# Pooling edges from gathered rows, and the mixer's instructions in another order

## The chip, the cores and the metric

One core of one Trainium2 chip runs the kernel. The core has engines that work side by side and each take their instructions strictly in the order of the program: TensorE (PE, matrix products into the eight PSUM banks), VectorE (DVE), ScalarE (ACT) and GpSimd (POOL). SyncE (SP) computes nothing here; its queue issues nearly all transfers between the device's memory (HBM) and the on-chip memory (SBUF). Engines wait for each other through semaphores. The metric is the device time of one execution in microseconds, lower is better. Times within the run are counted from the first instruction.

## The reference

A decoder trunk of two layers on 512 tokens with 1024 channels, all in float32. Layer 0 mixes tokens by pooling, layer 1 by sliding-window attention; a convolutional gated feed-forward network (FFN) follows each. The change lies in layer 0's mixer and in the start of its FFN:

```
def pool_mixer(h, w_pool, scale):      # h = rms_norm(x, mix_pre_g[0])
    # windows (2, 4, 8, 16), one for each group of 256 channels
    mean = (csum[:, 1:, sl] - csum[:, lo, sl]) / cnt      # causal trailing mean
    d = mean - hf[..., sl]
    y = einsum('bsgc,gcd->bsgd', d, w_pool)               # per group 256 x 256
    return y * scale

x = x + rms_norm(pool_mixer(h), mix_post_g[0])
f = conv_glu_ffn(rms_norm(x, ffn_pre_g[0]), ...)          # up-projection 1024 -> 2 * 2816 first
```

A token's trailing mean over up to 16 tokens reaches up to 15 tokens back, so the first tokens of a block of 128 need the last rows of the block before. These are the edges.

## The kernel before

The 512 tokens lie in four blocks (b = 0 to 3) of 128, the 1024 channels in eight chunks of 128; every chunk belongs to one of the four groups, two chunks to a group. The steps of the mixer are, for each block, with the names of the code and of the traces:

- **norm** (`mix_norm`): the mean square of x[b] in two halves (`ss_m`), three tiny steps on GpSimd that end in the reciprocal root (`rstd_end`, lines 285 and 286), and two VectorE products that write the normalised block `xm`.
- **pool** (`mix_pool`): for each chunk one float32 product of the block's rows with a banded 128 x 128 matrix (line 415), and for b > 0 one more product, 16 columns wide, of the *previous* block's whole 128 rows with the small edge matrix (line 416). Four chunks share a PSUM bank `pd`; ScalarE copies it to `d`. Block 0 has its own band and no edge (line 413).
- **map** (`mix_map`, line 426): eight products, 256 columns wide, with the pool weights `wp`, into two banks `my`. `wp` is the raw weight times the gain and the scale row (`mix_weights`, line 400); the scale row is spread over the partitions by two products with a matrix of ones (line 374).
- **post** (`mix_post`): the post norm and the sum into x[b], then **pre** (`mix_pre`): the norm for the FFN into `xn_f`, then **T** (`mix_T`, line 335): eight transposes, whose result is split into a high and a low part, `xTh` by ScalarE and `xTl` by VectorE.

The FFN's weights come in units of 1 MB (`load`, line 172, tile `raw`, two buffers). Each unit is split into a high part by ScalarE (`wh`) and a low part by VectorE (`wl`), for units 0 and 1 in quarters (`piece`, lines 214 and 220). The up-projection (`up`) makes every product three times (`mm3`, lines 342 to 344): high with high, high with low, low with high. In the mixer's stage it is made for two blocks at a time (256 columns), from the third unit on for all four (512 columns).

Before x arrives PE multiplies a matrix of ones with itself (`keep_busy`, line 369). SP loads, in this order: x[0] in two halves, the band for block 0, x[1], constants, the rest of the band, the pool weights in two halves, x[2], the post gain row (`mpost`), x[3], weight unit 0, the pre gain row (`fpre`, which takes the scale row's buffer), later constants, the convolution's constants, weight unit 1 (which takes the pool weights' buffer).

The order on PE, ScalarE, VectorE and GpSimd is that of the program text. SP alone is ordered by a planner from its own timing, among transfers whose buffers are free, the earlier in the text first. Buffers of one tag are handed out by the framework as they come free, which adds waits where a buffer is still in use.

Of the kernel before, what the change touches and what calls it, by code (L numbers as in the profile page):

```python
# [60 lines left out]
def _pieces(v, bits, n):  # L61
    out = []
    for _ in range(n - 1):
        q = 2.0 ** (math.floor(math.log2(v)) + 1 - bits)
        c = math.floor(v / q) * q
        out.append(c)
        v -= c
    out.append(float(np.float32(v)))
    return out


def build(nc, tc, ctx, a, out):
# [7 lines left out]
    def bank(name):  # L80
        return ps.tile([P, 512], F32, tag="ps", name=name)
# [20 lines left out]
    def gain_col(which, kc):  # L102
        o = C_GAIN + which * KC + kc
        return cst[:, o : o + 1]
# [58 lines left out]
    def load(i):  # L163
        if i in raws or i in ready or i >= N_UNITS:
            return
        r = pw.tile([P, 2048], F32, tag="raw", name=f"raw{i}", bufs=2)
        if U_K <= i < U_O:
            load_att(r, i, 0, 4)
            raws[i] = r
            return  # L170
        for o, src in source(i)[1]:
            nc.sync.dma_start(r[:, o : o + src.shape[1]], src)
        raws[i] = r
# [90 lines left out]
    def ahead(i, n=N_SLOTS):  # L264

        for k in range(i, i + n):
            split(k)
# [7 lines left out]
    def square(junk, src, ss, h, first):  # L275

        nc.scalar.activation(junk, src, AF.Square, scale=1.0 / math.sqrt(D), accum_out=ss[:, h : h + 1])  # L277
        if first:
            nc.gpsimd.tensor_scalar(ss[:, h : h + 1], ss[:, h : h + 1], EPS, None, ALU.add)  # L279

    def new_ss(name):
        return pc.tile([P, 4], F32, tag="ss", name=f"ss_{name}", bufs=6)

    def rstd_end(ss):
        nc.gpsimd.tensor_tensor(ss[:, 2:3], ss[:, 0:1], ss[:, 1:2], ALU.add)
        nc.gpsimd.tensor_tensor(ss[:, 3:4], ss[:, 2:3], mhalf, ALU.pow)
        return ss[:, 3:4]
# [8 lines left out]
    def halves(t):  # L296
        return [t[:, h * 512 : (h + 1) * 512] for h in range(2)]

    def post_norm(b, acc, grow, name, pool=None):
        if pool is None:  # L300
            ts_ = halves(pc.tile([P, D], F32, tag="t4", name=f"pt_{name}{b}", bufs=3))
        else:
            ts_ = [pool.tile([P, 512], F32, tag="qT", name=f"pt_{name}{b}_{h}", bufs=2) for h in range(2)]
        r = rstd_of(acc, ts_, f"p_{name}{b}")
        gs, xs = halves(grow), halves(x[b])
        for h in range(2):
            nc.vector.tensor_tensor(ts_[h], acc[h], gs[h], ALU.mult)
        for h in range(2):
            nc.vector.scalar_tensor_tensor(xs[h], ts_[h], r, xs[h], ALU.mult, ALU.add)
# [45 lines left out]
    nc.sync.dma_start(x[2], a["x"][2])  # L355
    post_row = bcast_row(a["mix_post_g"][0], "mpost0")
    nc.sync.dma_start(x[3], a["x"][3])
    load(U_IN[0])
    pre_row = bcast_row(a["ffn_pre_g"][0], "fpre0")
    load(U_IN[0] + 1)  # L360
    nc.sync.dma_start(cst[:, C_LATE:C_FREQ], a["cst"][:, C_LATE:C_FREQ])
    load_conv(0)
    scale_row = [bank(f"scale_row{h}") for h in range(2)]
    scratch = bank("scratch")

    def keep_busy(n):

        for _ in range(n):
            nc.tensor.matmul(scratch[:, :P], warm, warm, start=True, stop=True)

    keep_busy(13)

    for h in range(2):
        nc.tensor.matmul(scale_row[h], warm, row[:, h * 512 : (h + 1) * 512], start=True, stop=True)
    keep_busy(1)
    wp = pm.tile([P, 8, 256], F32, tag="wp", name="wp")
    xns, xnf = {}, {}

    def mix_norm(b):
        xm = pm.tile([P, D], F32, tag="xm", name=f"xm{b}", bufs=NB)  # L380
        ss = new_ss(f"m{b}")
        xs, junk = halves(x[b]), halves(xm)
        if b < 2:

            nc.scalar.activation(junk[0], xs[0], AF.Square, scale=1.0 / math.sqrt(D), accum_out=ss[:, 0:1])
            nc.vector.tensor_tensor_reduce(out=junk[1], in0=xs[1], in1=xs[1], scale=1.0 / D, scalar=EPS,
                                           op0=ALU.mult, op1=ALU.add, accum_out=ss[:, 1:2])
        else:
            for h in range(2):
                square(junk[h], xs[h], ss, h, h == 0)  # L390
        r = rstd_end(ss)
        for h in range(2):
            nc.vector.tensor_scalar(halves(xm)[h], halves(x[b])[h], r, None, ALU.mult)
        xns[b] = xm

    def mix_weights():
        pr = raws[U_POOL]
        for c in range(8):
            g = c // 2
            nc.vector.scalar_tensor_tensor(wp[:, c, :], pr[:, c * 256 : (c + 1) * 256], gain_col(0, c),  # L400
                                           scale_row[g // 2][:, (g % 2) * 256 : (g % 2 + 1) * 256], ALU.mult, ALU.mult)

    def mix_pool(b):
        d = pm.tile([P, D], F32, tag="d", name=f"d{b}", bufs=2)
        for h in range(2):
            pd = bank(f"pd{b}{h}")
            for k in range(4):
                c = h * 4 + k
                g = c // 2
                cs = slice(c * P, (c + 1) * P)  # L410
                o = pd[:, k * P : (k + 1) * P]
                if b == 0:
                    nc.tensor.matmul(o, xns[b][:, cs], band[:, g, P + EDGE :], start=True, stop=True)
                else:
                    nc.tensor.matmul(o, xns[b][:, cs], band[:, g, :P], start=True, stop=False)
                    nc.tensor.matmul(o[:, :EDGE], xns[b - 1][:, cs], band[:, g, P : P + EDGE], start=False, stop=True)
            nc.scalar.copy(d[:, h * 512 : (h + 1) * 512], pd)
        return d

    def mix_map(b, d):  # L420
        acc = [bank(f"my{b}{h}") for h in range(2)]
        for g in range(4):
            o = acc[g // 2][:, (g % 2) * 256 : (g % 2) * 256 + 256]
            for k in range(2):
                c = g * 2 + k
                nc.tensor.matmul(o, d[:, c * P : (c + 1) * P], wp[:, c, :], start=k == 0, stop=k == 1)  # L426
        return acc

    def mix_post(b, acc):
        post_norm(b, acc, post_row, "m0")  # L430

    def mix_pre(b):
        xnf[b] = pre_norm(b, pre_row, "f0")

    def mix_T(b):
        transpose_in(b, xnf[b], xT, "f0")

    u0, u1 = U_IN[0], U_IN[0] + 1
    mix_norm(0)
    mix_norm(1)  # L440
    d0 = mix_pool(0)
    mix_weights()
    mix_norm(2)
    d1 = mix_pool(1)
    acc0 = mix_map(0, d0)
    mix_post(0, acc0)
    mix_norm(3)
    acc1 = mix_map(1, d1)
    mix_pre(0)
    mix_post(1, acc1)  # L450
    d2 = mix_pool(2)
    piece(u0, 0)
    mix_T(0)
    mix_pre(1)
    piece(u0, 1)
    acc2 = mix_map(2, d2)
    piece(u0, 2)
    mix_post(2, acc2)
    d3 = mix_pool(3)
    mix_T(1)  # L460
    piece(u0, 3)
    mix_pre(2)
    acc3 = mix_map(3, d3)
    piece(u1, 0, defer=True)
    piece(u1, 1, defer=True)
    mix_post(3, acc3)
    while deferred:
        deferred.pop(0)()
    piece(u1, 2)
    piece(u1, 3)  # L470
    mix_pre(3)

    def start0():
        yield 0, (0, 2)
        mix_T(2)
        yield 1, (0, 2), (0,)
        mix_T(3)
        ctx_mix.close()
        yield 1, (0, 2), (1,)
        ahead(U_IN[0])  # L480
        rope_tables()
        yield 0, (2, 4)
        yield 1, (2, 4)


    sin_t = pc.tile([P, NB, 32], F32, tag="sin", name="sin_t")
# [29 lines left out]
        nc.scalar.activation(cos_t, ang, AF.Sin)  # L516


    def up(l, xT, j, accs, blks, sides=(0, 1)):
        hi, lo = slots[U_IN[l] + j]  # L520
        hi4 = hi.rearrange("p (k s c) -> p k s c", k=KC, s=2)
        lo4 = lo.rearrange("p (k s c) -> p k s c", k=KC, s=2)
        if j not in accs:
            accs[j] = [bank(f"u{l}_{j}_{s}") for s in range(2)]
        b0, b1 = blks
        for s in sides:
            o = accs[j][s][:, b0 * P : b1 * P].rearrange("p (b t) -> p b t", t=P)
            for k in range(KC):
# [694 lines left out]
```

## Time and profile before

| what | value |
|---|---|
| median of three runs | 910.92 us (910.71 to 912.18) |
| the profiled execution, its own time | 910.81 us |
| its span, first to last instruction | 909.0 us |
| PE busy | 900.4 us (99%) |
| DVE, ACT, POOL busy | 639.0, 457.9, 330.0 us |
| mean granted clock of PE | 0.999 |
| transfers over the span | 178.47 MB, mean 196 GB/s |

The page gives busy time by engine, the busy share of forty slices, the chain of work that ended last and the costliest groups. The end of a matmul in it is modelled, so a busy PE says less than its starts do: the distance from one start to the next is the time that a product takes. The views used below are the engines' rows in order of time (start, duration, engine, line, operation, tiles, count, and in brackets the idle time before with what ended it), the list of waits, the transfers from issue to landing, and busy time and granted clock in chosen stretches.

### The profile page before, as it was taken

What the parts mean: (1) busy time and instruction counts of PE and PEld (TensorE: products, weight loads), DVE (VectorE), ACT (ScalarE), POOL (GpSimd) and SP (SyncE); (2) the same over time, 40 slices, a digit from 0 to 9 for tenths busy, and PEclk for the clock granted to TensorE, in tenths of its full rate; (3) what the DMA queues carried; (4) which work ended last, traced back from release to release, by engine and by line L of the source; (5) the groups of instructions that cost most, each with busy time, mean ns of one, the idle gap of its engine ahead of it and who ended that gap; (6) DMA issues with size and microseconds to landing.
All of it is one profiled execution on the core that took longest, in us unless ns stands there. A gap on an engine that the chain in (4) does not pass through costs nothing.

```text
span 909.0 us, 12195 instructions
## 1 busy us (share of the span) xinstructions
PE 900.4 (99%) x4416; PEld 762.2 (84%) x4416; DVE 639.0 (70%) x949; ACT 457.9 (50%) x791; POOL 330.0 (36%) x360
## 2 busy tenths in 40 slices
PE   9999999999999999999999999999999999999996
PEld 8998888888888888888888889988888888888885
DVE  5987676676678679855988746655555555777897
ACT  5654444444444566545888635333333333455672
POOL 3418444444441003234655213544444444410031
PEclk9999999999999999999999999999999999999999
DMA  8257887888885666751211252555555555556562
GB/s 315 89 191 267 310 302 262 305 300 289 275 292 156 185 220 231 265 178 45 75 66 47 94 218 95 185 188 203 199 198 195 187 191 189 173 160 191 195 218 109
DMA packets 50207, 178.47 MB, mean 196 GB/s; under 512 B 5473, under 2 KB 13153, under 8 KB 42210
## 3 DMA queue, kind: packets, MB, share of 16 engines
q1 hardware_dynamic: 48272, 164.83, 52.3%
q10 hardware_dynamic: 1874, 12.85, 3.7%
q8 instruction: 35, 0.57, 0.3%
q14 instruction: 26, 0.21, 0.1%
HBM read 139.91 MB, written 37.75 MB: 195 GB/s over the span
## 4 chain that ended last, share of the span: by engine, by line
PE 96%; DVE 1%; DMA 1%; POOL 1%; ACT 0%; issue 0%; ACTq 0%; POOLq 0%; DVEq 0%
PE u L343 18%; PE u L342 18%; PE u L344 18%; PE dn L342 7%; PE dn L343 7%; PE dn L344 7%; PE op L342 2%; PE op L344 2%; PE op L343 2%; PE qp L343 2%; PE my L426 2%; PE qp L344 2%; PE qp L342 1%; PE pT L972 1%; DMA wl<-lo 1%; PE s L937 1%
## 5 line engine op out<-in xcount | busy, mean ns | idle before, releaser
L342 PE MATMUL u<-xTh_f,wh 128*128 128x512 f32 (+1 forms) x768 | 285.7, 372 | 0.0
L343 PE MATMUL u<-xTl_f,wh 128*128 128x512 f32 (+1 forms) x768 | 285.2, 371 | 0.0
L344 PE MATMUL u<-xTh_f,wl 128*128 128x512 f32 (+1 forms) x768 | 285.2, 371 | 0.0
L257 DVE TENSOR_TENSOR wl<-raw,wh 128x1024 fp32r<-128x1024 f32 (+1 forms) x158 | 206.6, 1338 | 33.0 <-ACT wh L256 32.6
L561 ACT ACTIVATE t<-u,conv 128x512 f32<-128x512 f32 x88 | 68.4, 780 | 250.3 <-PE u L344 219.4
L256 ACT CAST wh<-raw 128x1024 fp32r<-128x1024 f32 (+1 forms) x158 | 158.9, 1042 | 56.2 <-DMA raw<-t 41.4
L563 DVE SCALAR_TENSOR_TENSOR t<-u,conv,t 128x511 f32<-128x511 f32 x88 | 65.8, 747 | 147.7 <-ACT t L561 147.7
L342 PEld LDWEIGHTS u<-xTh_f,wh 128*128 128x128 f32 x768 | 144.6, 188 | 25.2
L344 PEld LDWEIGHTS u<-xTh_f,wl 128*128 128x128 f32 x768 | 144.6, 188 | 24.9
L343 PEld LDWEIGHTS u<-xTl_f,wh 128*128 128x128 f32 x768 | 144.6, 188 | 24.8
L582 POOL TENSOR_TENSOR G<-G,G 128x256 f32<-128x256 f32 x22 | 34.4, 1564 | 261.5 <-DVE G L577 261.5
L342 PE MATMUL dn<-wh,gh 128*128 128x512 f32 x276 | 107.6, 390 | 0.0
L344 PE MATMUL dn<-wh,gl 128*128 128x512 f32 x276 | 107.4, 389 | 0.0
L343 PE MATMUL dn<-wl,gh 128*128 128x512 f32 x276 | 107.4, 389 | 0.0
L279 POOL TENSOR_SCALAR ss_p_f<-ss_p_f 128x1 f32<-128x1 f32 x8 | 16.9, 2111 | 158.1 <-ACT dn L277 158.1
L564 DVE SCALAR_TENSOR_TENSOR t<-u,conv,t 128x510 f32<-128x510 f32 x88 | 65.9, 749 | 3.1
L344 PEld LDWEIGHTS dn<-wh,gl 128*128 128x128 f32 x276 | 51.8, 188 | 10.9
L342 PEld LDWEIGHTS dn<-wh,gh 128*128 128x128 f32 x276 | 51.8, 188 | 10.7
L343 PEld LDWEIGHTS dn<-wl,gh 128*128 128x128 f32 x276 | 51.8, 188 | 10.6
L948 ACT ACTIVATE P<-P,stat 128x256 f32<-128x256 f32 (+1 forms) x64 | 30.3, 476 | 11.4 <-DVE stat L945 11.3
L577 DVE TENSOR_TENSOR G<-t 128x512 f32<-128x512 f32 x44 | 32.3, 733 | 5.4 <-ACT t L571 1.0
L591 POOL TENSOR_TENSOR q<-q,q 128x512 f32<-128x512 f32 x22 | 33.0, 1502 | 4.3 <-PE tr_f L335 4.3
(193 smaller groups left out, 1380.6 us busy)
## 6 DMA issues: line engine op xcount, KB each, us to landing
raw<-in_ws_dram SPq DMA_DIRECT2D x46, 1024.0 KB, 5.0
q<-in_ws_dram SPq DMA_DIRECT2D x44, 512.0 KB, 6.1
raw<-t SPq DMA_DIRECT2D x24, 768.0 KB, 5.7
raw<-in_ws_dram SPq DMA_DIRECT2D x28, 512.0 KB, 4.8
t<-q SPq DMA_DIRECT2D x44, 256.0 KB, 2.8
t<-q SPq DMA_DIRECT2D x22, 512.0 KB, 2.8
hi<-h SPq DMA_DIRECT2D x12, 512.0 KB, 6.7
lo<-r SPq DMA_DIRECT2D x12, 512.0 KB, 5.9
```

Of the source, the lines that this page charges most:

```text
L256: nc.scalar.copy(hi[:, s], r[:, s])
L257: nc.vector.tensor_tensor(lo[:, s], r[:, s], hi[:, s].bitcast(F32), ALU.subtract)
L342: nc.tensor.matmul(acc, ah, bh, start=first, stop=False)
L343: nc.tensor.matmul(acc, ah, bl, start=False, stop=False)
L344: nc.tensor.matmul(acc, al, bh, start=False, stop=last)
L561: nc.scalar.activation(t, u, AF.Identity, bias=conv_col(l, ch, 3), scale=conv_col(l, ch, 2))
L563: nc.vector.scalar_tensor_tensor(t[:, 1:], u[:, : S - 1], conv_col(l, ch, 1), t[:, 1:], ALU.mult, ALU.add)
L564: nc.vector.scalar_tensor_tensor(t[:, 2:], u[:, : S - 2], conv_col(l, ch, 0), t[:, 2:], ALU.mult, ALU.add)
L577: nc.vector.tensor_tensor(g, tg, tv, ALU.mult)
L582: nc.gpsimd.tensor_tensor(s1, s1, G2[:, p, 2, :], ALU.add)
L591: nc.gpsimd.tensor_tensor(b22, b22, b12, ALU.subtract)
L948: nc.scalar.activation(Pt[:, h, 0:w], Pt[:, h, 0:w], AF.Exp, bias=nm[:, h : h + 1], scale=-1.0, accum_out=dn[:, h : h + 1])
```

## The change

**Edges.** The edge products of blocks 2 and 3 are replaced. A table `edge` of 128 x 8 x 16 is cleared on GpSimd and filled by eight small loads (16 rows of 16 numbers each), so that rows 16c to 16c+15 hold chunk c's edge matrix in chunk c's columns and zeros elsewhere. After block 1 is normalised, eight transfers within SBUF gather its last 16 rows, chunk c into rows 16c to 16c+15 of a tile `xe`; the same after block 2. One product of `xe` with four chunks' 64 columns of `edge` then adds the edges of four chunks to a bank at once. Block 1 keeps its eight narrow products. Only the first product into a bank of blocks 2 and 3 now starts it anew.

**Order.** The mixer's functions are taken apart into single steps, and a list of their names sets the order in which they are given out; as before, each engine takes its own in that order, and the transfers of `xe` go to SP. The first four up-projection parts (two units, two sides, two pairs of blocks, formerly 48 or 24 products at a time) are given out in quarters of six products. One filler product of PE behind the scale rows is gone; the scale rows are made one before and one behind the first half of pd0.

```diff
+MIXER = """
+    sqa0 sqa1 srow0 sqb0 rt0 xm00 xm01 sqb1 pd00 srow1 rt1 xm10 d00 xm11 pd01 wp3 d01 xe1 sqa2 wp2 pd10 wp5 sqb2
+    wp1 pd11 wp0 d10 wp7 wp4 sqa3 wp6 map00 eps2 psq00 rt2 xm20 xm21 eps3 peps0 ptt00 map01 xe2 psq01 map10 prt0
+    d11 wh00 ptt01 pd20 pst00 sqb3 map11 psq10 rt3 pst01 wl00 d20 nsq00 nsq01 psq11 pd21 wh10 xm31 xm30 wh01
+    map20 ptt10 d21 wh11 peps1 pd30 neps0 ptt11 nrt0 prt1 nst01 wh02 T01 psq20 nst00 pst10 T00 pd31 pst11 peps2
+    wl01 nsq10 neps1 wl10 map21 nsq11 d30 ptt20 th01 nrt1 tl01 map30 nst10 nst11 d31 T10 th00 wh12 psq21 T11
...
+    th30 th31 tl30 U1003 tl31 U0110 U1100 tl21 U0111 U1013 U1110 U0112 U0100 U1101 U0101 U0113 U0102 U1111 U0103
+    U1102 U1112 U1113 U1103
+"""
...
     nc.sync.dma_start(x[3], a["x"][3])
+    edge = pm.tile([P, KC, EDGE], F32, tag="edge", name="edge")
+    nc.gpsimd.memset(edge, 0.0)
+    for c in range(KC):
+        nc.sync.dma_start(edge[c * EDGE : (c + 1) * EDGE, c, :], a["band"][P - EDGE :, c // 2, P : P + EDGE])
     load(U_IN[0])
     pre_row = bcast_row(a["ffn_pre_g"][0], "fpre0")
     load(U_IN[0] + 1)
...
-    keep_busy(1)
...
+    def xe(b):
+        xes[b] = pm.tile([P, P], F32, tag="xe", name=f"xe{b}", bufs=2)
+        for c in range(KC):
+            nc.sync.dma_start(xes[b][c * EDGE : (c + 1) * EDGE, :], xns[b][P - EDGE :, c * P : (c + 1) * P])
...
+    def pdb(b, h):
+        pd = pds[b, h] = bank(f"pd{b}{h}")
+        for k in range(4):
+            c = h * 4 + k
+            g, cs, o = c // 2, slice(c * P, (c + 1) * P), pd[:, k * P : (k + 1) * P]
+            if b == 0:
+                nc.tensor.matmul(o, xns[b][:, cs], band[:, g, P + EDGE :], start=True, stop=True)
+            else:
+                nc.tensor.matmul(o, xns[b][:, cs], band[:, g, :P], start=k == 0 or b - 1 not in xes, stop=False)
+                if b - 1 not in xes:
                     nc.tensor.matmul(o[:, :EDGE], xns[b - 1][:, cs], band[:, g, P : P + EDGE], start=False, stop=True)
+        if b and b - 1 in xes:
+            nc.tensor.matmul(pd.rearrange("p (k t) -> p k t", k=4)[:, :, :EDGE], xes[b - 1], edge[:, h * 4 : h * 4 + 4, :],
+                             start=False, stop=True)
...
+    def U(u, p, s, q):
+        if (u, p, s, q) == (0, 1, 0, 0):
+            ctx_mix.close()
+            ahead(u0)
+            rope_tables()
+        up(0, xT, u, accs, (2 * p, 2 * p + 2), (s,), range(2 * q, 2 * q + 2))
...
-    def up(l, xT, j, accs, blks, sides=(0, 1)):
+    def up(l, xT, j, accs, blks, sides=(0, 1), ks=range(KC)):
...
-    accs = ffn_start(0, xT, start0())
+    for step in MIXER.split():
+        name = step.rstrip("0123456789")
+        do[name](*map(int, step[len(name) :]))
```

In the list `sqa` and `sqb` are a norm's two squares, `eps` and `rt` its steps on GpSimd, `xm` its two products; `srow` a scale row, `wp` a weight chunk, `pd`, `d` and `map` the pool, its copy and the map; `psq`, `peps`, `prt`, `ptt`, `pst` the post norm, `nsq`, `neps`, `nrt`, `nst` the pre norm; `T`, `th`, `tl` the transposes and their split, `wh`, `wl` a quarter of a weight unit's split; U1010 is unit 1, first pair of blocks, side 1, quarter 0. The first digit of the others is the block or unit, the second the half or quarter. The functions of the steps that are not shown hold the same instructions as the functions that they replace.

More of the change, by code (lines that the diff above doesn't have):

```diff
@@ L371, in build @@
     keep_busy(13)
-    for h in range(2):
-        nc.tensor.matmul(scale_row[h], warm, row[:, h * 512 : (h + 1) * 512], start=True, stop=True)
-    keep_busy(1)
[L376 to L382, printed above, removed]
+    wp = pm.tile([P, 8, 256], F32, tag="wp", name="wp")
+    xns, xes, xnf, dts, pds, accm, pts, sss, trs, scale_row = ({} for _ in range(10))
@@ new lines, in build, with srow, square_half @@
+    accs = {}
+    u0 = U_IN[0]
+    def srow(h):
+        scale_row[h] = bank(f"scale_row{h}")
+        nc.tensor.matmul(scale_row[h], warm, row[:, h * 512 : (h + 1) * 512], start=True, stop=True)
+    def square_half(name, b, h, new, src):
+        if h == 0:
+            pts[name, b] = new()
+            sss[name, b] = new_ss(f"{name}{b}")
+        nc.scalar.activation(halves(pts[name, b])[h], src, AF.Square, scale=1.0 / math.sqrt(D),
+                             accum_out=sss[name, b][:, h : h + 1])
@@ L383, in mix_norm, with add_eps, new_xm, sqa @@
+    def add_eps(name, b):
+        ss = sss[name, b]
+        nc.gpsimd.tensor_scalar(ss[:, 0:1], ss[:, 0:1], EPS, None, ALU.add)
+    def new_xm(b):
+        xns[b] = pm.tile([P, D], F32, tag="xm", name=f"xm{b}", bufs=NB)
+        return xns[b]
+    def sqa(b):
+        square_half("m", b, 0, lambda: new_xm(b), halves(x[b])[0])
+    def sqb(b):
         if b < 2:
-            nc.scalar.activation(junk[0], xs[0], AF.Square, scale=1.0 / math.sqrt(D), accum_out=ss[:, 0:1])
-            nc.vector.tensor_tensor_reduce(out=junk[1], in0=xs[1], in1=xs[1], scale=1.0 / D, scalar=EPS,
-                                           op0=ALU.mult, op1=ALU.add, accum_out=ss[:, 1:2])
-        else:
-            for h in range(2):
-                square(junk[h], xs[h], ss, h, h == 0)
@@ L391, in mix_norm @@
[L391 to L415, printed above, removed]
-                    nc.tensor.matmul(o[:, :EDGE], xns[b - 1][:, cs], band[:, g, P : P + EDGE], start=False, stop=True)
-            nc.scalar.copy(d[:, h * 512 : (h + 1) * 512], pd)
-        return d
@@ L420, in mix_map @@
[L420 to L483, printed above, removed]
+            x1 = halves(x[b])[1]
@@ new lines, in db, with mapb, new_t4 @@
+    def db(b, h):
+        if h == 0:
+            dts[b] = pm.tile([P, D], F32, tag="d", name=f"d{b}", bufs=2)
+        nc.scalar.copy(halves(dts[b])[h], pds[b, h])
+    def mapb(b, h):
+        acc = accm[b, h] = bank(f"my{b}{h}")
+        for c in range(4 * h, 4 * h + 4):
+            g, k = divmod(c, 2)
+            o = acc[:, (g % 2) * 256 : (g % 2) * 256 + 256]
+            nc.tensor.matmul(o, dts[b][:, c * P : (c + 1) * P], wp[:, c, :], start=k == 0, stop=k == 1)
+    def new_t4(name):
+        return lambda: pc.tile([P, D], F32, tag="t4", name=name, bufs=3)
@@ new lines, in T, with of_xT, th, tl @@
+    def T(b, h):
+        pt = trs[b, h] = bank(f"tr_f{b}{h}")
+        for k in range(4):
+            kc = h * 4 + k
+            nc.tensor.transpose(pt[:, k * P : (k + 1) * P], pts["n", b][:, kc * P : (kc + 1) * P], ident)
+    def of_xT(i, b, h):
+        return xT[i][:, b, h * 4 : (h + 1) * 4, :].rearrange("p k t -> p (k t)")
+    def th(b, h):
+        nc.scalar.copy(of_xT(0, b, h), trs[b, h])
+    def tl(b, h):
+        nc.vector.tensor_tensor(of_xT(1, b, h), trs[b, h], of_xT(0, b, h).bitcast(F32), ALU.subtract)
@@ L522, in up @@
         lo4 = lo.rearrange("p (k s c) -> p k s c", k=KC, s=2)
[L523 to L524 removed]
         b0, b1 = blks
         for s in sides:
+            if s not in accs.setdefault(j, {}):
+                accs[j][s] = bank(f"u{l}_{j}_{s}")
             o = accs[j][s][:, b0 * P : b1 * P].rearrange("p (b t) -> p b t", t=P)
[L528 removed]
+            for k in ks:
                 mm3(o, hi4[:, k, s, :], lo4[:, k, s, :],
```

34 lines of the change are left out of this document (33 added, 1 removed).

## The prediction

> **What bounds the kernel now.** I read the page first: busy shares, then the chain of waits.
>
> ```profile
> PE 900.4 (99%) x4416; PEld 762.2 (84%) x4416; DVE 639.0 (70%) x949; ACT 457.9 (50%) x791; POOL 330.0 (36%) x360
> ...
> PE 96%; DVE 1%; DMA 1%; POOL 1%; ACT 0%; issue 0%; ACTq 0%; POOLq 0%; DVEq 0%
> ```
>
> TensorE (PE) sets the end almost everywhere, so whatever the mixer's stage gains or loses on PE should reach the end undiminished. A busy PE is modelled, so I looked for its waits in the first 75 us, where all of the change lies, and then at its order of time.
>
> ```profile
> PE scratch L369 <- DVE warm L85: 1.0, 1, 1.0
> ```
> ```profile
> 1.04 5.51 PE L369 MATMUL scratch<-warm 128*128 128x128 f32 x26 [1.04 <-DVE warm L85]
> ...
> 8.10 0.38 PE L369 MATMUL scratch<-warm 128*128 128x128 f32 x2
> 8.32 1.95 PE L413 MATMUL pd<-band,xm 128*128 128x128 f32 x16
> 10.11 0.39 PE L415 MATMUL pd<-band,xm 128*128 128x128 f32 x2
> ...
> 13.60 7.15 PE L426 MATMUL my<-wp,d 128*128 128x256 f32 x32
> 20.59 0.38 PE L415 MATMUL pd<-band,xm 128*128 128x128 f32 x2
> ...
> 24.08 1.07 PE L335 MATMUL tr_f<-cst,xn_f 128*128 128x128 f32 x8
> ```
>
> The columns are start, duration, engine, line, operation, tiles and the number of records; a float32 product leaves two records. After the first start PE waits for nothing. So a new order cannot win by filling holes: there are none. Only work taken away can, and every new wait in PE's queue is a loss.
>
> **Part one: the edges.** Block 0 has no edge: 16 records, 8 products, from 8.32 to 10.11, 0.224 us each. Block 2 has 8 pairs of one 128-wide and one 16-wide product from 20.59 to 24.08, 0.44 a pair. The narrow product therefore costs 0.22, as much as the wide one. Blocks 2 and 3 lose 16 narrow products and get four that are 64 wide. No row shows 64 columns, but the neighbours on both sides, 16 and 128, stand at 0.22, so I take 0.22 (between 0.21 and 0.23 moves nothing). Gain: 12 x 0.22 = 2.65 us. The dropped filler product is 8.10 to 8.32: 0.22. Together **-2.87 us**, if no operand is late.
>
> **Part two: 24 more transfers on SP's queue.** Eight small loads of the edge table stand right behind x[3], ahead of the first weight unit (u0); eight gathers of block 1's last rows (xe1) and eight of block 2's (xe2) follow. What SP does today:
>
> ```profile
> 2.33 0.61 SPq L350 DMA_DIRECT2D x<-in_x_dram  x1
> 2.98 0.43 SPq L352 DMA_DIRECT2D cst<-in_cst_dram  x1
> 3.45 0.55 SPq L353 DMA_DIRECT2D band<-in_band_dram  x1
> 4.04 1.09 SPq L172 DMA_DIRECT2D raw<-in_ws_dram  x2
> 5.18 0.44 SPq L355 DMA_DIRECT2D x<-in_x_dram  x1
> 5.67 0.45 SPq L271 DMA_DIRECT2D mpost<-in_mix_post_g_dram  x1
> 6.16 0.65 SPq L357 DMA_DIRECT2D x<-in_x_dram  x1
> 6.90 0.53 SPq L172 DMA_DIRECT2D raw<-in_ws_dram  x1
> 8.30 0.33 SPq L271 DMA_DIRECT2D fpre<-in_ffn_pre_g_dram  x1
> 8.67 0.48 SPq L361 DMA_DIRECT2D cst<-in_cst_dram  x1
> 10.54 0.33 SPq L111 DMA_DIRECT2D conv<-in_cst_dram  x1
> 13.91 21.99 SPq L172 DMA_DIRECT2D raw<-in_ws_dram  x2
> ```
> ```profile
> SPq L111 <- DMA raw<-in_ws_dram: 1.4, 1, 1.4
> ```
> ```profile
> raw<-in_ws_dram SPq DMA_DIRECT2D x1, 1024.0 KB, 12.2
> ...
> mpost<-in_mix_post_g_dram SPq DMA_DIRECT2D x1, 512.0 KB, 8.9
> ...
> fpre<-in_ffn_pre_g_dram SPq DMA_DIRECT2D x1, 512.0 KB, 12.1
> ...
> conv<-in_cst_dram SPq DMA_DIRECT2D x1, 88.0 KB, 10.4
> ...
> raw<-in_ws_dram SPq DMA_DIRECT2D x1, 1024.0 KB, 4.7
> ...
> freq<-in_cst_dram SPq DMA_DIRECT2D x1, 16.0 KB, 2.2
> ```
> ```profile
> 6.91 0.63 ACT L385 ACTIVATE xm<-x 128x512 f32<-128x512 f32 x1 [2.78 <-DMA x<-in_x_dram]
> ...
> 13.11 0.63 ACT L277 ACTIVATE xm<-x 128x512 f32<-128x512 f32 x1 [2.21 <-DMA x<-in_x_dram]
> ...
> 8.61 0.88 DVE L393 TENSOR_SCALAR xm<-x,ss_m 128x512 f32<-128x512 f32 x2 [1.01 <-POOL ss_m L286]
> ...
> 10.65 3.22 DVE L400 SCALAR_TENSOR_TENSOR wp<-raw,cst,scale_row 128x256 f32<-128x256 f32 x8 [1.16 <-DMA raw<-in_ws_dram]
> ```
>
> Two things are to be seen. The conv load shares no tile with the pool weights (raw), yet SP held it 1.4 us until their first half landed at 10.5. Counted along the queue it is the eighth transfer after that half; u0 (6.90) is the eighth after x[1], which landed at 6.9. I read this as **at most eight transfers under way**: each waits until the one eight places before it has landed. And a small transfer lands behind the big ones before it: conv, 88 KB, took 10.4 us, while 16 KB on a quiet queue took 2.2.
>
> The seven rows of transfers are x count, KB of one and us from issue to landing; the 12.2 is u0's, the 4.7 that of the next unit, issued alone at 35.6.
>
> With these two the new queue can be walked. Landings now: x[2] 13.1, mpost 5.67 + 8.9 = 14.6, u0 6.90 + 12.2 = 19.1, and x[3], the first third of the bytes between these two, 16.1. Edge loads 1 to 8 wait for x[1] (6.9), cst, band, the two raw halves (10.5 and later), x[2] (13.1), mpost (14.6) and x[3] (16.1). SP is in order, so u0 stands behind the eighth and goes out at 16.5 instead of 6.90; by the quiet 4.7 us it lands at 21.2. fpre follows 1.3 later at 22.5 and, past cst (taken at 22.9), conv 0.6 after fpre at 23.1 (distances as now: 19.1, 20.4, 20.9). The first four gathers of xe1 go out by 19; the fifth waits for u0 (21.2), the sixth for fpre, the seventh for cst, the eighth for conv (23.1). It goes out at 23.3 and lands 2.2 later: **25.5**. Block 1's rows themselves are ready by 9.5, so the queue alone makes it late.
>
> PE comes to the first gathered product early: my starts at 13.60 - 0.22 = 13.4, three halves of map at 1.75 (13.60 to 20.59 is four) end at 18.6, four wide products later it is 19.5. It waits 25.5 - 19.5 = **6.0 us**, with all its queue behind it: map11, pd21, map20 and every U part are listed later, none can overtake.
>
> The price of a gather is bounded from below by its rows being ready at 9.5 plus 2.2, 11.7: no wait. From above, by the second weight unit u1 (13.91 now) slipping ahead of the gathers on SP: u1 lands 2.4 after conv, 25.5, the eighth gather waits for it and lands at 27.7: 8.2 us. I take 25.5, since the walk uses the code's order throughout.
>
> **Part three: the rest of the order.** u0 at 21.2 makes ScalarE, which comes to the first weight cast shortly after 18, wait there; behind it stand block 3's square, block 1's post square and d20, the copy of pd20. PE's own wait for the gather covers that. Without it four steps of 0.6 would end at 23.6, and map20 would be asked for at 19.7 + 1.75 + 1.1 = 22.6: 1.0 us. Clearing the edge table is one of GpSimd's first instructions, where it has nothing else to do. xe2's last gather waits for u1 (about 28.2) and lands at 30.4; PE, held first, gets to it at 25.5 + 0.2 + 1.75 + 1.1 + 1.75 + 0.9 = 31.2, so it costs nothing more. The U parts come in quarters: the same products, no cost. Unit 0 is now complete four quarters (4 x 0.72 = 2.9 us) before the stage's end, not 5.8:
>
> ```profile
> 56.60 1.43 ACT L561 ACTIVATE t<-u,conv 128x512 f32<-128x512 f32 x2
> ...
> 65.31 2.89 DVE L257 TENSOR_TENSOR wl<-raw,wh 128x1024 fp32r<-128x1024 f32 x2
> ```
>
> From the first activation to the split of unit 3 it is 68.2 - 56.6 = 11.6 us; started 2.7 before the stage's end it is done 8.9 after it, and PE wants unit 3 one unit (48 x 0.23 = 10.9 us) after. Two us of cover remain: cost nothing.
>
> **Sum.** -2.87 + 6.0 = +3.1. The profiled execution took 910.81 (span 909.0 and 1.8 around it; the median shown is 910.92), so **913.9 us**.
>
> **Rivals.**
> 1. *The gathers are in time: 907.9, faster.* If the planner of SP's queue puts the gathers before u0, or the limit of eight is looser than one clear wait lets me say, PE never waits and the whole -2.87 stays. For it: rows ready at 9.5, ten us ahead. Against it: conv's wait, and its 10.4 us to landing.
> 2. *Only the ring holds them: 909.4.* Behind conv without the limit, xe1 lands at 21.0: a wait of 1.5.
> 3. *The wait also cools PE: 916.4.* The first 26 records of scratch took 5.51 us, 0.21 each; the 16 records from 8.32 to 10.11, of the same shape, stand 0.11 apart. So PE starts at half rate and needs some 5 us of work. At the end of the run it falls back (columns: stretch, its length, busy time of PE, PEld, DVE, ACT and POOL, PE's granted clock, transfers):
>
> ```profile
> 900.00:902.00 2.00, 1.79 (x8) 1.13 (x7) 1.97 (x4) 0.72 (x2) 0.80 (x2) 1.00 0.00 0
> 902.00:904.00 2.00, 0.00 (x0) 0.00 (x0) 1.87 (x3) 0.72 (x2) 0.54 (x1) 1.00 0.35 131
> ...
> 907.00:909.00 2.00, 0.00 (x0) 0.00 (x0) 0.00 (x0) 0.00 (x0) 0.00 (x0) 0.53 0.33 125
> ```
>
> PE's work ends at 901.8, and a mean of 0.53 over the last stretch is the half clock from 907.1 on: 5.3 us of idleness did it once. A wait of 6.0 may do it too; 5 us at half rate lose 2.5. The Trainium skill, TensorE: Matmul & The Clock Gate, section "What's actually happening", speaks against the change here: an idle window of about 3.4 us drops the clock to half, and a busy one of the same length restores it. By that rule a wait of 6.0 us holds a whole window about three times in four, and the loss would be 1.7 to 3.4 us. The trace has no wait of PE between its first and last matmul, so it cannot say which.
> 4. *u1 goes first: 916.1,* from the 8.2 us above, or 918.6 with the clock's loss.
> 5. *The order stalls without the gathers: 909 to 911.* GpSimd's tiny steps can be held up:
>
> ```profile
> 13.91 0.22 POOL L279 TENSOR_SCALAR ss_m<-ss_m 128x1 f32<-128x1 f32 x1 [5.33 <-ACT xm L277]
> ...
> 40.75 2.24 POOL L279 TENSOR_SCALAR ss_n_f<-ss_n_f 128x1 f32<-128x1 f32 x1 [2.08 <-ACT xn_f L277]
> ```
>
> The same step takes 0.22 in one place and 2.24 in another; 2 us on block 2's or 3's norm would eat most of the gain.
>
> **Chances.** The forecast 0.33; rival 3 0.19; rival 4 0.10; rival 1 0.27; rival 2 0.05; rival 5 0.06. About 1.8 us (0.2%) is what a measurement tells from no change. So faster 0.27 (rival 1), same 0.11 (rivals 2 and 5), slower 0.62 (the rest). The range is 907.6 to 917.8, from the full gain to the cooled clock; the forecast's own is 912.8 to 915.
>
> **What would show it.** In the changed trace: the 64-wide products at 0.22; u0 issued near 16.5, not 6.90, and each SP issue just behind the landing eight places before; the last xe1 gather landing near 25.5; one PE wait of some 6 us before the first gathered product, and no other above 0.5. Wrong if that wait is missing or the gathers stand ahead of u0 in SP's order; half right if the records behind the wait are 0.21 apart instead of 0.11.

## The result, and the profile after

The changed kernel takes **919.4 us** (median of five runs, 918.5 to 920.7) against 910.92: a ratio of 1.0093, 95% interval 1.0079 to 1.0107. It is slower, and by more than the range on record allowed (917.8). The profiled execution is the slowest of the five, 920.7 us with a span of 918.9, 9.9 us above the span of before.

The page of the changed kernel, busy time and the chain of waits:

```profile
PE 900.2 (98%) x4390; PEld 761.0 (83%) x4390; DVE 639.3 (70%) x949; ACT 458.2 (50%) x791; POOL 328.7 (36%) x361
...
PE 91%; DVE 3%; DMA 2%; issue 1%; ACT 1%; POOL 1%; SPq 0%; DVEq 0%; POOLq 0%; ACTq 0%
```

PE has 26 records fewer (4416 to 4390: twelve products and one filler, two records each), yet its busy time is nearly that of before, and its share of the chain fell from 96 to 91%. Where the 9.9 us lie is seen from one mark, the start of the first 512-wide up-projection product, which ends the stage that the change touches:

```profile
70.96 0.40 PE L357 MATMUL u<-xTh_f,wh 128*128 128x512 f32 x1
```

and the same product before:

```profile
61.06 0.40 PE L342 MATMUL u<-xTh_f,wh 128*128 128x512 f32 x1
```

From it to the end of the span it is 918.9 - 70.96 = 847.9 us, and before 909.0 - 61.06 = 847.9. So all of the loss is in the first 71 us and the rest takes the same time. PE's waits in the first 80 us (tiles, what ended the wait, us in total, times, longest):

```profile
PE pd L454 <- DMA xe<-xm: 9.0, 1, 9.0
...
PE pd L450 <- DVE xm L430: 0.9, 1, 0.9
PE my L467 <- DVE wp L439: 0.2, 1, 0.2
```

PE's rows in order of time around the long one:

```profile
19.39 1.05 PE L450 MATMUL pd<-band,xm 128*128 128x128 f32 x8
29.42 0.66 PE L454 MATMUL pd<-edge,xe 128*128 128x64 f32 x2 [8.98 <-DMA xe<-xm]
29.87 3.73 PE L467 MATMUL my<-wp,d 128*128 128x256 f32 x8
33.39 1.91 PE L450 MATMUL pd<-band,xm 128*128 128x128 f32 x8
35.10 0.37 PE L454 MATMUL pd<-edge,xe 128*128 128x64 f32 x2
35.31 1.95 PE L467 MATMUL my<-wp,d 128*128 128x256 f32 x8
37.09 1.05 PE L450 MATMUL pd<-band,xm 128*128 128x128 f32 x8
```

The first gathered product waits 8.98 us. Behind it the same work goes at half speed: eight mapping records take 3.73 us, then 1.95; eight band records 1.91, then 1.05. The stretches show the clock (columns: stretch, length, busy time of PE, PEld, DVE, ACT and POOL, PE's granted clock, transfers, GB/s):

```profile
20.00:25.00 5.00, 0.44 (x4) 0.25 (x3) 2.38 (x5) 1.81 (x5) 1.26 (x3) 0.99 0.92 360
25.00:30.00 5.00, 0.58 (x3) 0.61 (x4) 0.78 (x2) 0.00 (x0) 0.00 (x0) 0.50 0.36 133
30.00:35.00 5.00, 5.00 (x17) 4.28 (x17) 0.64 (x2) 3.18 (x9) 1.48 (x5) 0.50 0.05 12
35.00:40.00 5.00, 5.00 (x40) 4.79 (x39) 4.50 (x8) 4.62 (x12) 1.81 (x5) 0.98 0.00 0
```

A mean of 0.99 is 0.1 us at half rate (twice the missing share, times the length), 0.98 is 0.2: the clock was at half from 24.9 to 35.2. PE worked from 29.42 on, so 5.7 us of work at half rate cost 2.9.

The terms add up: -2.9 for the products and the filler, +9.0, +0.9 and +0.2 of waits, +2.9 of clock, 10.1 us against 9.9 measured. One thing is not in this sum: by the clock's records in the traces, PE's clock rose to full at 4.4 us here and at 6.0 in the run of before (the 26 filler records at the start take 4.8 us here and 5.5 there). That is worth up to 0.8 us, so such a sum is good to about that much.

SP's queue, the transfers that it issued (start, duration of the row, line, tiles, count):

```profile
7.61 9.13 SPq L378 DMA_DIRECT2D edge<-in_band_dram  x8
16.78 0.83 SPq L187 DMA_DIRECT2D raw<-in_ws_dram  x1
17.73 0.36 SPq L286 DMA_DIRECT2D fpre<-in_ffn_pre_g_dram  x1
18.13 0.43 SPq L382 DMA_DIRECT2D cst<-in_cst_dram  x1
18.66 0.62 SPq L187 DMA_DIRECT2D raw<-in_ws_dram  x1
19.33 0.45 SPq L126 DMA_DIRECT2D conv<-in_cst_dram  x1
19.82 13.42 SPq L435 DMA_DIRECT2D xe<-xm  x16
```

The eight edge loads, 16 rows each, hold SP for 9.1 us, and u0 goes out at 16.78. The row at 18.66 is u1, the second weight unit. It stands **ahead** of conv and of all sixteen gathers. The buffer that it takes, that of the pool weights, was free by then: VectorE had read it by 12.72 + 2.44 = 15.2.

```profile
12.72 2.44 DVE L439 SCALAR_TENSOR_TENSOR wp<-raw,cst,scale_row 128x256 f32<-128x256 f32 x6 [0.36 <-DMA raw<-in_ws_dram]
```

What u1 did is in the transfers issued from 18.5 to 19.6, and then in the last two gathers of block 1, issued from 26.5 to 28.2 (count, KB of one, us to landing):

```profile
raw<-in_ws_dram SPq DMA_DIRECT2D x1, 1024.0 KB, 8.4
...
conv<-in_cst_dram SPq DMA_DIRECT2D x1, 88.0 KB, 7.9
```
```profile
xe<-xm SPq DMA_DIRECT2D x2, 8.0 KB, 1.7
...
27.05 1.14 SPq L435 DMA_DIRECT2D xe<-xm  x2
```

u1 lands at 18.66 + 8.4 = 27.0. The seventh gather, eight transfers behind it in the queue, goes out at 27.05; the eighth lands at 29.3, and at 29.42 PE goes on. Other issues follow a landing eight places before in the same way: the third edge load goes out at 10.11 (the rest of the band lands at 10.10), the fourth gather at 22.12 (u0, 22.10), the fifth at 24.07 (`fpre`, 24.05). The list of SP's waits names the same transfers:

```profile
SPq L435 <- DMA raw<-in_ws_dram: 2.2, 2, 1.8
...
SPq L435 <- DMA fpre<-in_ffn_pre_g_dram: 1.4, 1, 1.4
```

### The profile page after: what moved, and what is told of

Its sections match the earlier page's. It is cut to its first block, busy times and chain, and to the rows that moved or that the text cites. A ratio compares the mean times of both kernels' runs of the same rounds, so it can differ in the third digit from the quotient of the medians.

```text
span 918.9 us, 12182 instructions
## 1 busy us (share of the span) xinstructions
PE 900.2 (98%) x4390; PEld 761.0 (83%) x4390; DVE 639.3 (70%) x949; ACT 458.2 (50%) x791; POOL 328.7 (36%) x361
## 4 chain that ended last, share of the span: by engine, by line
PE 91%; DVE 3%; DMA 2%; issue 1%; ACT 1%; POOL 1%; SPq 0%; DVEq 0%; POOLq 0%; ACTq 0%
PE u L357 17%; PE u L358 17%; PE u L359 17%; PE dn L359 6%; PE dn L357 6%; PE dn L358 6%; DMA raw<-in_ws_dram 2%; PE op L357 2%; PE op L359 2%; PE qp L357 2%; PE qp L359 2%; PE op L358 2%; PE qp L358 2%; PE my L467 2%; PE pT L1012 1%; DVE wl L272 1%
## 5 line engine op out<-in xcount | busy, mean ns | idle before, releaser
L272 DVE TENSOR_TENSOR wl<-raw,wh 128x1024 fp32r<-128x1024 f32 (+1 forms) x158 | 206.4, 1338 | 31.8 <-ACT wh L271 31.5
L358 PEld LDWEIGHTS u<-xTl_f,wh 128*128 128x128 f32 x768 | 144.6, 188 | 24.9
```

What stands on the lines that cost most here:

```text
L272: nc.vector.tensor_tensor(lo[:, s], r[:, s], hi[:, s].bitcast(F32), ALU.subtract)
L358: nc.tensor.matmul(acc, ah, bl, start=False, stop=False)
```

## The experiments

Nine kernels were run beside the two. In the table, "mark" is the start of the first 512-wide product in the profiled execution, the waits are PE's in the first 80 us, and "half clock" is the time that the granted clock stood at half behind the wait. Each ratio is to runs of the kernel before on the same chip (medians 911.09, 910.99 and 910.87); order_only was run again as order_only_b for its trace, because the profiled one of its ten executions took 4770 us, and its mark is that of order_only_b. A mark is that of one execution, and can differ from the medians by more than a microsecond.

| kernel | median us | ratio (95%) | mark | wait for xe | half clock |
|---|---|---|---|---|---|
| before | 910.92 | | 61.06 | none | none |
| after | 919.4 | 1.0093 (1.0079 to 1.0107) | 70.96 | 9.0 | 10.2 |
| order_only | 911.29 | 1.000 (0.9991 to 1.001) | 61.14 | none | none |
| no_gather | 908.68 | 0.997 (0.9957 to 0.9983) | 58.58 | none | none |
| no_gather_8 | 910.18 | 0.9989 (0.998 to 0.9999) | 61.55 | none | none |
| one_load | 916.49 | 1.0059 (1.0043 to 1.0076) | 65.32 | 4.6 | 3.4 |
| warm | 917.07 | 1.0062 (1.0047 to 1.0077) | 67.79 | 1.3 | none |
| old_order | 917.22 | 1.0065 (1.0051 to 1.0079) | 67.10 | 7.0 | 6.8 |
| u1_behind | 916.44 | 1.006 (1.0046 to 1.0074) | 67.27 | 5.6 | 6.8 |
| mixed | 909.56 | 0.9981 (0.9972 to 0.999) | 59.85 | 0.9 | none |
| mixed_late | 909.17 | 0.998 (0.9971 to 0.9989) | 59.72 | 0.7 | none |

**order_only: the order without the gathers.** All 16 narrow products stay; table, loads and gathers are gone.

```diff
-    sqa0 sqa1 srow0 sqb0 rt0 xm00 xm01 sqb1 pd00 srow1 rt1 xm10 d00 xm11 pd01 wp3 d01 xe1 sqa2 wp2 pd10 wp5 sqb2
-    wp1 pd11 wp0 d10 wp7 wp4 sqa3 wp6 map00 eps2 psq00 rt2 xm20 xm21 eps3 peps0 ptt00 map01 xe2 psq01 map10 prt0
+    sqa0 sqa1 srow0 sqb0 rt0 xm00 xm01 sqb1 pd00 srow1 rt1 xm10 d00 xm11 pd01 wp3 d01 sqa2 wp2 pd10 wp5 sqb2
+    wp1 pd11 wp0 d10 wp7 wp4 sqa3 wp6 map00 eps2 psq00 rt2 xm20 xm21 eps3 peps0 ptt00 map01 psq01 map10 prt0
...
-    edge = pm.tile([P, KC, EDGE], F32, tag="edge", name="edge")
-    nc.gpsimd.memset(edge, 0.0)
-    for c in range(KC):
-        nc.sync.dma_start(edge[c * EDGE : (c + 1) * EDGE, c, :], a["band"][P - EDGE :, c // 2, P : P + EDGE])
```

> The new order alone: no edge table, no gathers; blocks 2 and 3 keep their narrow edge products. Queue theory (the eight lanes and the gathers' late landing are the whole loss): PE's work is that of before less one filler product, no wait of PE above 1 us, about 910.7 (910.0 to 911.7). Order theory (quarters, the late unit 0 or GpSimd's held-up steps cost much of the 8.5 us): 913 or more, with the waits spread over the stage.

> The new order alone once more, for its profile: no wait of PE above 1 us, the first 512-column product near 61.

911.29 against 911.09: the order alone moves nothing that these runs can tell (0.9991 to 1.001). In order_only_b (912.86) the mark is at 61.14 and PE waits 0.5 us once, for block 1's rows. So rival 5, an order that stalls by itself, is out, and the loss belongs to the edges.

**no_gather and no_gather_8: the new products without the gathers.** In both the gathered tile is cleared instead of filled, so the edges of blocks 2 and 3 are left out of the result; the products over it are all made. no_gather also loads the table in one transfer, laid out beforehand; no_gather_8 keeps the eight loads.

```diff
-        for c in range(KC):
-            nc.sync.dma_start(xes[b][c * EDGE : (c + 1) * EDGE, :], xns[b][P - EDGE :, c * P : (c + 1) * P])
+        nc.gpsimd.memset(xes[b], 0.0)
```

and in no_gather alone:

```diff
-    nc.gpsimd.memset(edge, 0.0)
-    for c in range(KC):
-        nc.sync.dma_start(edge[c * EDGE : (c + 1) * EDGE, c, :], a["band"][P - EDGE :, c // 2, P : P + EDGE])
+    nc.sync.dma_start(edge, a["edge"])
```

> The tile of gathered rows is cleared on GpSimd instead of being gathered (so the edges of blocks 2 and 3 are left out of the result), and the edge table comes in one load laid out beforehand; all products and the order stay. Queue theory: the wait before the first gathered product is gone, the stage is worth its full 2.87 us: 908.0 (907.5 to 909.0). Product theory (the 64-wide product into strided columns is dear, or the order stalls by itself): 911 or more.

> As the kernel without gathers (their tile cleared, the edges of blocks 2 and 3 left out), but with the eight table loads: weight unit 0 goes out near 16.5 and lands near 21.5. This prices the eight table loads by themselves: ScalarE waits in the first weight cast, block 2's copy d20 is late for map20 by about 1 us: 909.5 (908.7 to 910.5).

no_gather is 2.4 us faster than before (908.68 against 911.09). PE's rows of no_gather, one half of block 2:

```profile
19.01 1.05 PE L447 MATMUL pd<-band,xm 128*128 128x128 f32 x8
19.90 0.33 PE L451 MATMUL pd<-edge,xe 128*128 128x64 f32 x2
20.07 1.95 PE L464 MATMUL my<-wp,d 128*128 128x256 f32 x8
```

Four band products take 0.89, the 64-wide one 0.17 to the next start, 1.06 in all; before, four pairs took 1.75. The gain of the products is real: 4 x 0.69 = 2.7 us.

With the eight loads the time is 910.18, so the eight loads by themselves take 1.5 us of it back. Its rows on ScalarE and PE:

```profile
22.08 0.62 ACT L229 CAST wh<-raw 128x512 fp32r<-128x512 f32 x1 [3.22 <-DMA raw<-in_ws_dram]
```
```profile
24.43 1.99 PE L466 MATMUL my<-wp,d 128*128 128x256 f32 x8 [1.14 <-ACT d L459]
```

u0 is late, ScalarE waits for it with its first weight cast, the copy d20 stands behind that cast, and PE waits 1.14 us with map20. The prediction had named this chain, at 1.0 us. The marks lie further apart than the medians, 61.55 against 58.58: besides the waits listed, PE's transposes and maps between 27 and 35 us are stretched (for example 4.06 us for sixteen mapping records against 3.67), and what stretches them stays open.

**one_load: the eight edge loads become one**, the gathers stay as they are (the second of the two diffs above, on the changed kernel).

> The edge table in one load instead of eight, the sixteen gathers as they are. Queue theory: weight unit 0 goes out near 8 us instead of 16.8, but the last three gathers of block 1 still stand behind weight unit 1 and land near 26 instead of 29.3: PE waits about 6 us, 914 if the clock holds, 917 if it falls. If the gathers themselves are slow (small rows, 0.6 us of issue each): the wait stays near 9 us and the time near 919.

916.49. u0 goes out at 8.54 instead of 16.78, and the wait is still 4.6 us (about 6 was expected). u1 again slips in, between the fifth and sixth gather (issued 19.11, landed 24.1); the sixth is held until `fpre` lands (20.8), and the last gather lands behind u1, at 24.8. How the wait divides between the two causes was not tried. Most of the loss is in any case not the edge loads': 5.4 of 8.5 us remain. The wait, and the clock behind it:

```profile
24.89 0.63 PE L452 MATMUL pd<-edge,xe 128*128 128x64 f32 x2 [4.57 <-DMA xe<-xm]
```
```profile
25.00:30.00 5.00, 5.00 (x22) 4.34 (x23) 0.48 (x1) 3.01 (x9) 1.31 (x5) 0.66 0.05 10
```

0.34 x 2 x 5 = 3.4 us at half rate, 1.7 lost. A wait of 4.6 was enough to halve the clock. The profiled run is the shortest of the four (914.94); PE's mean granted clock was 0.996 in it and 0.993 to 0.995 in the others, which points to more time at half clock in these.

**warm: the wait stays, PE is kept busy in it** by 34 products of the matrix of ones, put ahead of the first gathered product.

```diff
+        if (b, h) == (2, 0):
+            keep_busy(34)
         if b and b - 1 in xes:
```

> The changed kernel with 34 filler products (34 x 0.22 = 7.6 us) put on PE between the four wide products of block 2's first half and its gathered product. Clock theory (about a third of the loss is the half clock from 24.9 to 35.2): the wait is as long but the clock holds, 916.5 (915.8 to 917.3). If the clock is no part of the loss: 919.4, or more where the filler outlasts the wait.

917.07, 2.3 us less than the changed kernel, and the mark 3.2 earlier, though the gathered product starts at nearly the same time (29.04 against 29.42):

```profile
19.95 7.76 PE L389 MATMUL scratch<-warm 128*128 128x128 f32 x68
29.04 0.41 PE L456 MATMUL pd<-edge,xe 128*128 128x64 f32 x2 [1.33 <-DMA xe<-xm]
29.28 1.95 PE L469 MATMUL my<-wp,d 128*128 128x256 f32 x8
```

Behind it the eight mapping records take 1.95 and not 3.73. The 2.3 us are the clock's share by itself.

**old_order: the new edges in the order of before**, each gather step right behind its block's norm.

```diff
-    sqa0 sqa1 srow0 sqb0 rt0 xm00 xm01 sqb1 pd00 srow1 rt1 xm10 d00 xm11 pd01 wp3 d01 xe1 sqa2 wp2 pd10 wp5 sqb2
...
+    srow0 srow1 sqa0 sqb0 rt0 xm00 xm01 sqa1 sqb1 rt1 xm10 xm11 xe1 pd00 d00 pd01 d01 wp0
+    wp1 wp2 wp3 wp4 wp5 wp6 wp7 sqa2 sqb2 eps2 rt2 xm20 xm21 xe2 pd10 d10 pd11 d11
...
```

> The edge change alone: eight table loads and sixteen gathers on SP as in the changed kernel, the steps given out in the order of before. Queue theory: weight unit 1 stands before the gathers again, the last one lands near 29; PE comes to it about 1.3 us later than in the changed kernel (four halves of map lie ahead instead of three): a wait of 7 to 8 us with the half clock, 918 (917 to 919.5). Order theory (the new order is what hurts): 912 or less.

917.22; the wait is 7.0 and not 9.0:

```profile
28.64 0.66 PE L455 MATMUL pd<-edge,xe 128*128 128x64 f32 x2 [6.99 <-DMA xe<-xm]
```

PE comes 1.2 us later to the product here (21.65 against 20.44), and the gathers land 0.8 earlier. The clock falls all the same. Neither of the two orders removes the loss.

**u1_behind: one load moved.** u1 is asked for behind block 1's gathers; all else is the changed kernel.

```diff
     pre_row = bcast_row(a["ffn_pre_g"][0], "fpre0")
-    load(U_IN[0] + 1)
     nc.sync.dma_start(cst[:, C_LATE:C_FREQ], a["cst"][:, C_LATE:C_FREQ])
     load_conv(0)
...
             nc.sync.dma_start(xes[b][c * EDGE : (c + 1) * EDGE, :], xns[b][P - EDGE :, c * P : (c + 1) * P])
+        if b == 1:
+            load(U_IN[0] + 1)
```

> The changed kernel with one load moved: weight unit u1 is asked for right after the eight gathers of block 1's rows, where the changed kernel had it ahead of the conversion table and of all the gathers. Theory (the unit that slipped ahead is what made the wait 9.0 us rather than 6.0): the walk of the prediction holds again, the last gather is issued when the conversion table lands, near 23 to 24.5, and lands 25 to 26.5; TensorE comes to the gathered product near 20.4, so the wait is 5 to 6 us; the clock still falls near 24.9, for one step of 3.4 us, so 1.7 us more; first 512-wide product near 66.5 to 67.5 against 70.96, time 914.5 to 916.5. If the wait comes from the gathers themselves and not from u1: wait 8 to 9 us, 919. If the second set of gathers now becomes late because u1 lies in front of it: a new wait on the second gathered product, 917 to 919.

The conversion table of this text is the conv load. SP's rows, and its last three gathers of block 1 (issued from 23.1 to 24.5):

```profile
16.48 0.46 SPq L187 DMA_DIRECT2D raw<-in_ws_dram  x1
17.05 0.36 SPq L286 DMA_DIRECT2D fpre<-in_ffn_pre_g_dram  x1
17.46 0.43 SPq L381 DMA_DIRECT2D cst<-in_cst_dram  x1
17.94 0.71 SPq L126 DMA_DIRECT2D conv<-in_cst_dram  x1
18.75 5.70 SPq L434 DMA_DIRECT2D xe<-xm  x8
24.54 0.53 SPq L187 DMA_DIRECT2D raw<-in_ws_dram  x1
```
```profile
xe<-xm SPq DMA_DIRECT2D x3, 8.0 KB, 1.7
```

The eight gathers are done issuing at 24.4, and the last lands at 25.6; the prediction's walk had 25.5. The transfers before them also land where the walk put them: u0 at 21.4, `fpre` 22.6, conv 23.2 (walk: 21.2, 22.5, 23.1). PE and the clock:

```profile
25.71 0.66 PE L455 MATMUL pd<-edge,xe 128*128 128x64 f32 x2 [5.62 <-DMA xe<-xm]
```
```profile
25.00:30.00 5.00, 4.29 (x12) 3.61 (x13) 0.04 (x1) 1.90 (x6) 0.96 (x3) 0.50 0.64 221
30.00:35.00 5.00, 5.00 (x33) 4.79 (x33) 4.36 (x7) 4.60 (x12) 1.32 (x3) 0.85 0.02 3
```

With u1 out of the way the wait is 5.6 us, and the time falls from 919.4 to 916.44. So u1's place in the queue is worth 3.0 us. But the clock stays at half until 31.5 (0.15 x 2 x 5 = 1.5 us into the last stretch), not for the one step of 3.4 us that was expected: 5.8 us of work at half rate, 2.9 lost. The mark is 67.27; -2.9 + 0.7 + 5.6 + 2.9 = 6.3 above before, 6.2 measured.

**mixed: block 1's rows gathered from another queue.** One load of the table; block 1's eight gathers are issued by GpSimd, block 2's by SP.

```diff
-            nc.sync.dma_start(xes[b][c * EDGE : (c + 1) * EDGE, :], xns[b][P - EDGE :, c * P : (c + 1) * P])
+            (nc.gpsimd if b == 1 else nc.sync).dma_start(xes[b][c * EDGE : (c + 1) * EDGE, :],
+                                                         xns[b][P - EDGE :, c * P : (c + 1) * P])
```

> The edge table in one load, block 1's gathers issued from GpSimd's queue (lanes and rings of its own), block 2's from SP; order and products as in the changed kernel. Queue theory: block 1's rows are there by 16, PE reaches them at 19.9 without a wait; block 2's last gather stands behind weight unit 1 (23.4) and lands about 25.6, when PE comes (25.6): a wait of 0.5 at most; 908.7 (908.0 to 909.6), faster than before. If gathers from another queue also land behind SP's bulk (21 or later): a wait of 1.5 or more, 910 or more.

909.56: faster than before (0.9972 to 0.999), by 1.4 us. PE's row, GpSimd's row of the eight issues, and these gathers among the transfers of the first 40 us:

```profile
21.11 0.41 PE L452 MATMUL pd<-edge,xe 128*128 128x64 f32 x2 [0.94 <-DMA xe<-xm]
```
```profile
10.51 4.11 POOL L433 DMA_DIRECT2D xe<-xm  x8 [0.84 <-DVE xm L428]
```
```profile
xe<-xm POOLq DMA_DIRECT2D x8, 8.0 KB, 6.0
```

GpSimd issued its eight from 10.5 to 14.6, without a wait between them, and they still took 6 us (median) to land, among the bulk loads on SP's queue. The last one landed at 20.9; I had expected them to be in SBUF by 16, and PE to find them there without a wait. What the other queue saved is the standing in line. The Trainium skill, DMA: Bandwidth & Descriptors, section "Issuing engines are not separate DMA queues", says that transfers of all issuing engines run on the same 16 DMA engines and interleave, and that another issuer saves the sequencer's time only. The 6.0 us fit its first half; in this kernel, though, the time saved on the issuer is what counts, since SP's gathers waited there for landings (in the changed kernel the seventh until 27.05).

**mixed_late: the same, with the gathered half block behind one more mapping step.**

```diff
-    d11 wh00 ptt01 pd20 pst00 sqb3 map11 psq10 rt3 pst01 wl00 d20 nsq00 nsq01 psq11 pd21 wh10 xm31 xm30 wh01
+    d11 wh00 ptt01 pst00 sqb3 map11 pd20 psq10 rt3 pst01 wl00 d20 nsq00 nsq01 psq11 pd21 wh10 xm31 xm30 wh01
```

> The mixed kernel (table of edges in one load, block 1's rows gathered by GpSimd's queue, block 2's by SP's) with one step moved: the gathered product of block 2's first half is given out after block 1's second mapping product instead of before it, so that TensorE has 1.9 us of other work while the last gather lands. If the 0.9 us wait is all that the gathers still cost: no wait on the gathered rows, first 512-wide product near 59.0 against 59.85, time 908.4 to 909.0, which is that of the kernel without gathers (908.68). If moving it only shifts the wait to the copy of that half and the mapping behind it: 909.5, as mixed.

909.17 (0.9971 to 0.9989), not to be told from mixed. The wait on block 1's rows is gone as expected, but one comes up at block 3's half, for block 2's rows:

```profile
26.66 0.41 PE L452 MATMUL pd<-edge,xe 128*128 128x64 f32 x2 [0.69 <-DMA xe<-xm]
```

Those are SP's gathers. The last of them goes out at 24.85, when u1 has landed, and lands at 26.6. The wait moved on to the next late transfer; 909.17 beats the kernel before and the changed one. It is 0.5 us above no_gather's 908.68, which the intervals do not tell apart.

## Why the prediction was wrong, step by step

- **The direction and the limit of eight: right.** Waits of PE for the gathers, set by SP's queue with eight transfers under way, made the kernel slower, and no_gather without them is faster. u0 went out at 16.78 (16.5 forecast).
- **The gain of the products, -2.87: right in size.** The 64-wide product took 0.17 rather than 0.22. no_gather measures -2.4 by its medians and -2.5 by its mark, with 0.6 us of a new small wait in it (for block 1's rows, which PE now reaches before they are normalised). The prediction held that no wait but the gather's would exceed 0.5; in the changed kernel this one was 0.9, and PE came to the first gathered product at 20.4, not 19.5.
- **The failed step: "I take 25.5, since the walk uses the code's order throughout."** The walk's order, with u1 behind conv and behind block 1's gathers, is not the code's. In the code `load(U_IN[0] + 1)` stands ahead of conv and of the gathers, as the diff of u1_behind shows; behind conv is where SP's rows of before have u1 (13.91), after VectorE had read the pool weights out of its buffer. In the changed kernel that buffer had been read by 15.2, before u0 went out at 16.78. So nothing held u1 back, and the planner, which takes the earlier in the text among transfers whose buffers are free, put it ahead of conv and of the gathers. (This reason is read from the times; the runs show the place in the queue and what it costs.) The last gather landed at 29.3, the wait was 9.0 and not 6.0. u1_behind restores the order that the walk assumed and gives what the walk gave: 25.6 and a wait of 5.6. u1's place costs 919.4 - 916.4 = 3.0 us.
- **The second term missing from the sum: the clock.** The forecast had PE's clock untouched by a wait of 6.0 and left its fall to rival 3. With the order as assumed and a wait of 5.6 the time is 916.44; rival 3 said 916.4. That the two agree so closely is partly luck: the wait was 0.4 shorter than rival 3's, the clock's loss 0.4 larger (2.9 for 2.5), and the small wait of 0.7 for block 1's rows was not in it. So even with the right order the forecast would have been 2.5 us low. warm shows the clock's share in the changed kernel, 919.4 - 917.1 = 2.3.
- **Rival 4 is what happened**, in its form with the clock's loss: 918.6 against 919.4. u1 landed at 27.0 instead of 25.5 and the last gather at 29.3 instead of 27.7, while PE came 0.9 later, so the wait was 9.0 instead of 8.2. That form lay outside the range, which ended at 917.8 though it was one of the text's own cases.
- **u0's delay costs nothing behind the gathers' wait: right here.** Its cost without that cover was given as 1.0 us; no_gather_8 measured a wait of 1.1, and 1.5 us in the medians.
- **Rivals 1, 2 and 5: wrong.** The gathers were not in time, and the order by itself is 1.000. Nor was it the ring alone, for then the wait would have been 1.5 and not 9.0. mixed, whose gathers for block 1 do not wait in SP's line, comes near what rival 2 describes: the last lands at 20.9 (rival 2: 21.0), and PE waits 0.9.

Two things stay open. The eight gathers from GpSimd need 6 us while bulk loads run, where a gather from SP on an emptier queue needs 1.7. That bulk traffic is the cause is argued from the time at which each was issued, not tried; and the trace of mixed puts GpSimd's transfers into a queue of another kind (packets, MB, share of 16 engines), which may have a part in it:

```profile
q1 hardware_dynamic: 3519, 7.47, 51.8%
q0 software_dynamic: 256, 0.07, 0.8%
```

And the two repairs that leave all gathers on SP, one load of the table and u1 behind the gathers, were each run alone, not together.

## What to carry to other kernels

Before adding small transfers to a queue, list what the queue holds at that moment, the loads that a planner may slip ahead included, and let each new transfer wait for the landing of the one eight places before it: twenty-four transfers of 1 to 8 KB cost more here than the 2.7 us of products that they saved. The waits of PE of 4.6 us and more had a second price here, the half clock behind them; those of 1.3 us and less had none, and nothing in between was run. A forecast with such a wait in it should carry both. If rows must be gathered, a queue without bulk loads in line did it for a wait of 0.9 us, and a table that one load can bring should not take eight.

## What the runs showed of the hardware

By the clock's records in the traces, the half clock behind a wait lasted 3.4 us (one_load), 6.8 (u1_behind, old_order) or 10.2 (the changed kernel): multiples of 3.41. In these runs the clock had come to full at 4.2 to 4.5 us and fell at 24.7 to 24.9, 20.5 us or six such steps later, whatever the wait's own start (20.1 to 21.7). A wait of 4.6 us that ended just before a step's end cost one step; one of 5.6 us that ended 1.0 us into the next step cost two. The Trainium skill, TensorE: Matmul & The Clock Gate, section "What's actually happening", gives this rule: a free-running window of 3413 ns, an idle one halves the clock, a busy one restores it. The traces agree, and they show how busy a step must be: one in which u1_behind's PE worked for 2.4 us of 3.4 did not restore the clock, and one in which old_order's PE worked for 3.1 did. The price is half of what is left of the half clock when PE goes on: 1.7 us in one_load, 1.6 in old_order, 2.9 in u1_behind and in the changed kernel.

A queue of transfers is not only issue time: in the changed kernel SP took 9.1 us over the eight edge loads, seven of them held until the one eight places before had landed, and in mixed GpSimd issued its eight gathers, eight times as large, in 4.1 us without such a wait.
